# A hybrid decoder layer whose instruction order is planned at build time: other costs in the planner for POOL's inversion, the landing of stores and transfers in flight

## The chip, the cores and the metric

The kernel runs on one core of one Trainium2 chip. The metric is the device time of one execution in microseconds (us). A core has five engines with queues of their own: PE (matmuls; PEld in the profile is its weight load), DVE and ACT (elementwise work), POOL (elementwise work on SBUF alone) and SP, which here issues every transfer. Each engine works through its instructions in the order in which the program holds them and waits at semaphores for the others. So the order in which the instructions are written down decides what waits.

## The reference

One layer over 4096 tokens of width 1024: an RMS norm, one input projection `u = h @ w_in`, two groups of heads on its columns, a gate, an output projection with the residual, and a final RMS norm.

```
S_t = diag(a_t) S_{t-1} + k_t^T v_t ;  o_t = q_t S_t                              # GLA, 4 heads, 64 x 128
S_t = S_{t-1} (diag(w_t) - kk_t^T (a_t * kk_t)) + v_t^T k_t ;  y_t = S_t r_t       # RWKV-7, 8 heads, 64 x 64
x = x + concat(gla_out * silu(gg), (y + bonus) * silu(rg)) @ w_out
```

The inputs of the projections are float32; the kernel computes them with pairs of float16 numbers.

## The kernel before, in words

**Tiling.** The tokens go through in 8 blocks of 512. A projection (`proj`) is 24 float16 matmuls of 128x512: 8 slices of the width, three times, for the products of high and low halves of x and weight. Weights come as 29 column tiles of w_in and 8 of w_out. In the first block each tile is loaded as float32, its maximum is found (ACT `wo<-x`, then a transpose on PE, `bank<-ident,amW`), it is scaled and split into two float16 halves (`split_w`, line 604), and the halves are stored to DRAM (`wdr<-wo`, 512 KB; `wdr<-wr` and `wdr<-wg` for the first twelve). From the thirteenth tile on, the split works in two buffers `hls` (`wo` in the profile), so a store must have landed before the tile after the next can be split. Later uses load the halves from `wdr` into `wr`, `wg` or `wo` (256 KB each).

**RWKV.** Each block has four units, each of two heads, 32 units u = 4*b + p in all. `rwkv_ab` (line 833) projects, builds DD and bk on DVE, and multiplies them within chunks of 64 tokens (`bank<-DD,bk`); the masked products go to DD and Nb. DD and Nb have two buffers (`NBUF = 2`, line 525): unit u writes those of unit u-2, and line 881 lets it go on only when the scan of u-2 is written down. Then comes an inversion of triangular 32x32 blocks: four stores of 32 KB (`nd<-Nb`), four loads of 128 KB (`f<-nd`) that bring the rows to their partitions, 31 steps of two operations on POOL (`tm<-Tc,f`, `Tc<-Tc,tm`, lines 923 and 925), four stores `td<-Tc` and four loads `Nb<-td`. The last unit has its steps on DVE. `rwkv_i` (line 980) finishes the inverse with a transpose on DVE (`Ta<-Nb`) and small matmuls (`bank<-Ta,Nb`). `rwkv_c` (line 1002) is the scan over the 8 chunks of a unit: three float32 matmuls a chunk into `ch`, with ACT and DVE between them, then y (`y<-DD,sv`, `y<-Nb,uv`). `rwkv_d` (line 1046) normalises y; small rows go through DRAM to be spread over partitions (`bcast`, line 692: `bcda`, `bcdb`, `bcdc`, ...).

**The rest.** GLA's heads run beside that (`gla_proj`, `gla_pair`), `x_block` (line 739) prepares the next block's x, with its squares added up on POOL (`xacc`), and `out_block` (line 1240) does the output projection of a finished block.

**The order.** Every operation is recorded, not issued, by `Engine` (line 367, the issuing call is line 408, which is why every row of the profile has this line). Eight generators, one for each of the streams above, are run against a clock of costs (`run`, line 428), which fixes the buffers and the dependencies. Then a list scheduler plans all five engines: `forward` (line 245) goes through the steps by rank with a duration and a lag for each, `backward` (line 306) makes ranks from the far end, and this is repeated 13 times; the order with the earliest end by its own account is kept. All steps are then issued in the order of their planned starts. `cost` (line 334) has the durations for POOL ("G"), DVE ("V") and ACT ("S"). A transfer ("D") occupies its issuer for 0.63 us, begins 1.28 us later, lasts its bytes at 360 GB/s, and its reader may start a lag after that, with `SPARE` (0.45 us) on top.

In the built program the transfers use eight semaphores in turn, and each transfer waits until the eighth before it has landed.

Of the kernel before, what the change touches and what calls it, by code (L numbers as in the profile page):

```python
# [18 lines left out]
DRAM = bass.MemoryType.DRAM  # L19
# [62 lines left out]
def hymba_kernel(ctx, tc, xT, wt, wg, wo, wua, gup, pk, ck, out):  # L82
# [7 lines left out]
    big = ctx.enter_context(tc.tile_pool(name="big", bufs=1))  # L90
# [97 lines left out]
    steps, wkey, rkey, wlast, readers = [], {}, {}, {}, {}  # L188
# [56 lines left out]
    def forward(rank):  # L245


        wait, can, free = {e: [] for e in "VSGTD"}, {e: [] for e in "VSGTD"}, dict.fromkeys("VSGTDH", 0.0)
        pes, tab, run = Array(), 0, None
        left, ready, start = [len(s.on) for s in steps], [0.0] * len(steps), [0.0] * len(steps)  # L250
        end = [0.0] * len(steps)
        for s in steps:
            if not s.on:
                heapq.heappush(wait[s.eng], (0.0, s.n))

        def soonest(e):
            t = pes.free if e == "T" else free["H" if e == "D" else e]
            return t if can[e] else max(t, wait[e][0][0]) if wait[e] else 1e18

        for _ in steps:  # L260
            e = min("VSGTD", key=soonest)
            t = soonest(e)
            while wait[e] and wait[e][0][0] <= t:
                n = heapq.heappop(wait[e])[1]
                heapq.heappush(can[e], (rank[n], n))
            if e == "T":
                x = next((x for x in can[e] if run and x[1] == run.n), None)
                x = x or min(heapq.nsmallest(12, can[e]), key=lambda x: x[0] - 2.0 * (steps[x[1]].form == pes.form))
                run = steps[x[1]].next
                can[e].remove(x)  # L270
                heapq.heapify(can[e])
            else:
                x = can[e][0]
                soon = []
                while e in "VS" and wait[e] and wait[e][0][0] <= t + 0.15:
                    r, n = heapq.heappop(wait[e])
                    soon.append((r, n))
                    if rank[n] + 2 * (r - t) < x[0]:
                        x = (rank[n] + 2 * (r - t), n)
                for y in soon:  # L280
                    if y[1] != x[1]:
                        heapq.heappush(wait[e], y)
                if x is can[e][0]:
                    heapq.heappop(can[e])
            s = steps[x[1]]
            t, d = max(t, ready[s.n]), s.d
            start[s.n] = t
            if e == "T":
                start[s.n], d = pes.put(t, d, s.cols, s.tiles)
                end[s.n] = start[s.n] + d  # L290
            elif e == "D":
                free["H"], free["D"] = t + 0.63, max(t + 1.28, free["D"]) + d
                end[s.n] = free["D"]
            else:
                if s.tab is not None:
                    d, tab = d + 1.3 * (s.tab != tab), s.tab
                end[s.n] = free[e] = t + d
            for m in s.to:
                lat = m.on[s]
                ready[m.n] = max(ready[m.n], start[s.n] if lat is None or lat < 0 else end[s.n] + lat)  # L300
                left[m.n] -= 1
                if not left[m.n]:
                    heapq.heappush(wait[m.eng], (ready[m.n], m.n))
        return start, end
# [29 lines left out]
    def cost(eng, op, ins, n, o, acc=False):  # L334

        big = [a for a in ins if math.prod(a.shape[1:]) > 1 or n == 1]
        few = len(ins) - len(big)
        psum = any(a.space == PSUM for a in ins)
        if eng == "V":
            fast = len(big) == 1 and not psum and op in ("tensor_scalar", "tensor_copy", "tensor_scalar_mul", "tensor_scalar_max")  # L340
            if op == "tensor_tensor_scan":
                return 0.068 + n / 480
            half = o.shape[0] < 128
            runs = 0.0
            if op == "copy_predicated":
                runs = 0.135 if half else 0.013
            elif n == 64:
                runs = 0.126
            elif n == 256 and half:
                runs = 0.122 if op == "transpose" else 0.09  # L350
            elif n == 512 and half:
                runs = 0.115
            elif op == "tensor_scalar" and few > 1:
                runs = 0.06
            return 0.068 + 0.06 * (few > 0) + n / (1920 if fast else 960) + runs
        if eng == "G":
            if op == "memset":
                return 0.135 + n * 0.52 / 960
            return 0.14 + 0.07 * few + n * (2.13 if len(big) > 1 else 0.95) / 960 + 0.34 * (n == 8)
        if n <= 4:  # L360
            return 0.1 if n == 1 else 0.03
        if n == 64 and o.shape[0] == 64:
            return 0.231 if psum else 0.147
        d = (0.052 if psum else 0.094) + n / 1200 + 0.09 * (few > 0) + 0.11 * (o.shape[0] < 128)
        return d + (0.035 + 0.05 * (few > 1) if few and psum and n > 128 else 0.02 * (few > 0)) + 0.1 * acc

    class Engine:
# [5 lines left out]
        def __getattr__(self, op):  # L373
            f = getattr(self.eng, op)

            def call(*a, **kw):
                aps = [x for x in list(a) + list(kw.values()) if isinstance(x, bass.AP)]
                cols, tiles, tab, lag = 0, None, None, 0.2
                assert aps
                if aps:  # L380
                    o, ins, outs = aps[0], aps[1:], aps[:1]
                    n = max(math.prod(x.shape) // max(x.shape[0], 1) for x in aps)
                    if self.name == "T":
                        r = ins[-1] if op == "matmul" else ins[0]
                        n = math.prod(r.shape) // r.shape[0] if op == "matmul" else r.shape[0]
                        n *= (4 if op == "matmul" else 2) if r.dtype == F32 else 1
                        k = [(x.start_partition() // 32, (x.start_partition() + x.shape[0] + 31) // 32) for x in (ins[0], o)]
                        k.append((1 + (op == "matmul")) * (r.dtype == F32))
                        d, lag, cols, tiles = n / 2400 + 0.0025, 0.25, n * r.shape[0] / 128, k
                        t0 = account("T", o, ins, d, lag, cols, tiles)  # L390
                    elif self.name == "D":
                        b = math.prod(o.shape) * (2 if o.dtype == F16 else 4)
                        d, lag = max(0.01, b / 3.6e5), 1.6 if ins[0].space == DRAM else 0.6
                        t0 = account("D", o, ins, d, lag)
                    else:
                        e = kw.get("accum_out")
                        ins = [x for x in ins if x is not e]
                        outs = [o] + ([e] if e is not None else [])
                        d = cost(self.name, op, ins, n, o, e is not None)
                        if op == "activation" and a[2] in (AF.Ln, AF.Exp, AF.Tanh):  # L400
                            tab = int(a[2] == AF.Ln)
                        load = 1.2 * (tab is not None and tab != table[0])
                        table[0] = table[0] if tab is None else tab
                        t0 = account(self.name, o, ins, d + load, lag)
                        if e is not None:
                            for k in parts(e):
                                ready[k] = (ready[parts(o)[0]][0] + 0.1, self.name)
                put(t0, self.name, d, lag, cols, tiles, tab, outs, ins, lambda: f(*a, **kw))  # L408

            return call  # L410
# [1064 lines left out]
    with tc.manual_schedule(engines={getattr(mybir.EngineType, e) for e in ("PE", "DVE", "Activation", "Pool", "SP")}):  # L1475
# [6 lines left out]
        start, end = forward([s.t0 for s in steps])  # L1482
        start, end = best = forward(backward(end))
        for _ in range(12):
            start, end = forward(backward(end))
            best = min(best, (start, end), key=lambda x: max(x[1]))
        start, end = best
# [65 lines left out]
```

## Time and profile before

| | us |
|---|---|
| median of 3 runs (2348.07 to 2359.25) | 2356.71 |
| the profiled execution | 2357.35 |
| its span, first to last instruction | 2355.5 |
| PE busy | 2245.6 |
| DVE busy | 1664.7 |
| ACT busy | 1251.0 |
| POOL busy | 842.1 |

The mean granted clock of PE is 0.979 of full speed. How to read the lines below: a group has the line, the engine, the operation, the tiles out<-in (buffer numbers left out), shapes, the count, then busy us and mean ns of one, then the engine's idle time just before it and what ended it. In a list of waits there follow total us, number of times and the longest. In a table by stretch each engine has busy us with its instructions, then the granted clock, the share of the transfer engines in use and GB/s. In the chain of waits a transfer's piece runs from issue to landing. SPq is SP's own queue.

### The profile page before, as it was taken

How to read it: one execution, taken by the hardware profiler on the slowest of the kernel's cores; microseconds unless marked ns; L12 is line 12 of the kernel's file. 1: busy time of each engine (PE TensorE's matmuls, PEld its weight loads, DVE VectorE, ACT ScalarE, POOL GpSimd, SP SyncE). 2: the span in 40 equal slices, each digit the busy share in tenths (PEclk: the TensorE clock that was granted, in tenths of full speed). 3: DMA queues.
4: the chain of work that ended last, by engine and by line, in shares of the span. 5: the costliest groups of instructions: out<-in, count | busy, mean ns of one | idle time of the engine just before them, and what ended most of it. 6: DMA issues, size and time to landing. Idle time of an engine off the chain costs nothing.

```text
span 2355.5 us, 52166 instructions
## 1 busy us (share of the span) xinstructions
PE 2245.6 (95%) x19432; PEld 1390.7 (59%) x19432; DVE 1664.7 (71%) x3737; ACT 1251.0 (53%) x3229; POOL 842.1 (36%) x2213
## 2 busy tenths in 40 slices
PE   6888999999999999999999999999999989999986
PEld 3556565556665666656575566655666556755643
DVE  7868768478764786757766787638877677676756
ACT  7566765454654655544654546535564455544442
POOL 3450333524334352235425342342514353321400
PEclk9989999999999999999999999999999999999989
DMA  6666545355334543345424553345533454334432
GB/s 195 204 217 213 158 154 157 113 169 152 103 106 125 179 151 93 109 137 174 141 85 121 175 160 97 102 133 173 153 94 106 123 184 137 97 118 127 130 86 76
DMA packets 275523, 325.46 MB, mean 138 GB/s; under 512 B 131732, under 2 KB 132932, under 8 KB 275268
## 3 DMA queue, kind: packets, MB, share of 16 engines
q1 hardware_dynamic: 275268, 322.13, 45.0%
q8 instruction: 152, 2.49, 0.4%
q14 instruction: 103, 0.84, 0.1%
HBM read 276.97 MB, written 45.05 MB: 137 GB/s over the span
## 4 chain that ended last, share of the span: by engine, by line
PE 68%; DVE 19%; DMA 5%; issue 3%; ACT 2%; POOL 2%; SPq 1%; DVEq 0%; ACTq 0%; POOLq 0%
PE bank L408 60%; PE ch L408 6%; PE y L408 2%; DVE DD L408 2%; DVE nta L408 2%; DVE bk L408 1%; POOL tm L408 1%; POOL Tc L408 1%; DVE mgg L408 1%; DVE mgr L408 1%; SPq L408 1%; DMA wdr<-wo 1%; DVE Nb L408 1%; DVE crs L408 1%; DVE sv L408 1%
## 5 line engine op out<-in xcount | busy, mean ns | idle before, releaser
L408 PE MATMUL bank<-x,wr 128*128 128x512 f16 x3264 | 803.1, 380 | 12.5 <-DVE rk L408 4.7
L408 POOL TENSOR_TENSOR tm<-Tc,f 128x60 f32<-128x60 f32 (+24 forms) x961 | 332.4, 346 | 762.3 <-DMA f<-nd 586.0
L408 PEld LDWEIGHTS <-wr 128*128 128x128 f16 x3264 | 317.0, 100 | 308.0 <-issue 21.4
L408 PE MATMUL bank<-x,wg 128*128 128x512 f16 x1536 | 389.6, 383 | 2.4 <-DMA wg<-wdr 2.0
L408 POOL TENSOR_TENSOR Tc<-Tc,tm 128x60 f32<-128x60 f32 (+24 forms) x961 | 341.6, 355 | 73.4
L408 PE MATMUL bank<-x,wo 128*128 128x512 f16 x1488 | 361.9, 384 | 0.6 <-ACT bk L408 0.6
L408 DVE SCALAR_TENSOR_TENSOR sv<-ch,PC,psd 64x64 f32<-64x64 f32 x448 | 126.2, 282 | 195.9 <-PE ch L408 191.0
L408 POOL TENSOR_TENSOR xacc<-xacc,xr 128x512 f32<-128x512 f32 x98 | 131.3, 1340 | 314.8 <-ACT xr L408 215.3
L408 PEld LDWEIGHTS <-wg 128*128 128x128 f16 x1536 | 148.5, 101 | 147.4 <-issue 11.6
L408 PEld LDWEIGHTS <-wo 128*128 128x128 f16 x1488 | 146.0, 101 | 139.9 <-issue 8.0
L408 PEld LDWEIGHTS <-x 128*128 128x128 f16 x3120 | 189.9, 100 | 27.6 <-issue 12.2
L408 PE MATMUL bank<-wg,x 128*128 128x128 f16 x3072 | 199.6, 222 | 4.5 <-DMA wg<-wdr 4.5
L408 ACT ACTIVATE psd<-sv,PC 128x128 f32<-128x128 f32 x256 | 102.2, 399 | 190.1 <-DVE sv L408 152.9
L408 ACT COPY uv<-ch 64x64 f32<-64x64 f32 x512 | 105.5, 206 | 120.5 <-PE ch L408 114.8
L408 ACT COPY us<-ch 64x64 f32<-64x64 f32 x512 | 105.3, 206 | 103.7 <-PE ch L408 93.3
L408 PEld LDWEIGHTS ch<-sv,DD 128*128 128x128 f32 x512 | 91.9, 192 | 49.3 <-DVE sv L408 20.3
L408 PEld LDWEIGHTS ch<-us,Nb 128*128 128x128 f32 x512 | 92.3, 192 | 40.0 <-ACT us L408 10.5
L408 PEld LDWEIGHTS ch<-uv,bk 128*128 128x128 f32 x512 | 92.4, 192 | 39.6 <-ACT uv L408 12.5
L408 PE MATMUL ch<-sv,DD 128*128 128x128 f32 x512 | 105.9, 289 | 8.7 <-DVE sv L408 6.6
L408 ACT ACTIVATE sa<-bank,mu_s 128x512 f32<-128x512 f32 x104 | 71.5, 688 | 73.5 <-PE bank L408 68.5
L408 PE MATMUL ch<-uv,bk 128*128 128x128 f32 x512 | 103.4, 284 | 4.1 <-ACT uv L408 4.0
L408 POOL MEMSET Tc<- 32x8 f32 (+1 forms) x160 | 23.7, 148 | 223.3 <-DMA td<-Tc 182.2
(332 smaller groups left out, 3670.9 us busy)
## 6 DMA issues: line engine op xcount, KB each, us to landing
wr<-wdr SPq DMA_DIRECT2D x256, 256.0 KB
wg<-wdr SPq DMA_DIRECT2D x184, 256.0 KB
xr<-in_xT_dram SPq DMA_DIRECT2D x176, 256.0 KB
wo<-wdr SPq DMA_DIRECT2D x128, 256.0 KB
f<-nd SPq DMA_DIRECT2D x128, 128.0 KB
x<-in_wt_dram SPq DMA_DIRECT2D x29, 512.0 KB
wdr<-wo SPq DMA_DIRECT2D x25, 512.0 KB
out_dram<-mgg SPq DMA_DIRECT2D x33, 256.0 KB
```

The lines of the kernel that those rows point to most:

```text
L408: put(t0, self.name, d, lag, cols, tiles, tab, outs, ins, lambda: f(*a, **kw))
```

## The change

Only the planner is changed; the generators that say what is computed are not.

- `cost`: an operation on POOL other than a memset takes 0.23 us instead of 0.14 ahead of its elements.
- The recording of a transfer: the lag after a store to DRAM was 0.6 us; it becomes 2.0 us for over 200 KB, 1.3 us where the last dimension is 32 (`nd<-Nb`, `td<-Tc`), and stays 0.6 us for the rest. The lag after a load from DRAM stays 1.6 us.
- `forward`: a transfer can't start before the eighth one ahead of it has ended, its lag included.

```diff
-        end = [0.0] * len(steps)
+        end, flight = [0.0] * len(steps), []
...
             elif e == "D":
+                if len(flight) > 7:
+                    start[s.n] = t = max(t, flight[-8])
                 free["H"], free["D"] = t + 0.63, max(t + 1.28, free["D"]) + d
                 end[s.n] = free["D"]
+                flight.append(end[s.n] + s.lag)
...
-            return 0.14 + 0.07 * few + n * (2.13 if len(big) > 1 else 0.95) / 960 + 0.34 * (n == 8)
+            return 0.23 + 0.07 * few + n * (2.13 if len(big) > 1 else 0.95) / 960 + 0.34 * (n == 8)
...
-                        d, lag = max(0.01, b / 3.6e5), 1.6 if ins[0].space == DRAM else 0.6
+                        d, lag = max(0.01, b / 3.6e5), 1.6 if ins[0].space == DRAM else 2.0 if b > 2e5 else 1.3 if o.shape[-1] == 32 else 0.6
```

The first and last of these reach the generators' run as well as the list scheduler; the limit on transfers is in `forward` alone.

## The prediction

> **What bounds the kernel now.** I read the totals of the page first, then busy time by stretch, then the waits of PE, and last SP and POOL, which the change is about.
>
> ```profile
> span 2355.5 us, 52166 instructions
> PE 2245.6 (95%) x19432; PEld 1390.7 (59%) x19432; DVE 1664.7 (71%) x3737; ACT 1251.0 (53%) x3229; POOL 842.1 (36%) x2213
> ```
>
> ```profile
> core 0: us, PE busy (x) PEld busy (x) DVE busy (x) ACT busy (x) POOL busy (x), PEclk, DMA share, GB/s
> 0.00:200.00 200.00, 162.66 (x1124) 95.10 (x1126) 157.38 (x442) 132.68 (x256) 82.21 (x179) 0.92 0.68 211
> 200.00:2200.00 2000.00, 1955.94 (x17214) 1217.87 (x17210) 1409.35 (x3044) 1064.88 (x2826) 738.53 (x1979) 0.99 0.45 135
> 2200.00:2355.50 155.50, 126.98 (x1104) 77.76 (x1102) 97.96 (x253) 53.49 (x149) 21.37 (x55) 0.90 0.28 83
> ```
>
> PE is the bound: it stands idle for 37.3 us in the first 200 us (200 less 162.66), 44.1 in the 2000 in the middle and 28.5 at the end, 109.9 in all. The granted clock costs something beside that: 8% of the 162.66 busy us of the start, 1% of the 1955.94, 10% of the 126.98, 45 us together. So a microsecond of PE idle goes with some 0.4 us of lower clock (45 by 109.9), and a change of order can win or lose only in these two sums. What ends PE's longer idle stretches:
>
> ```profile
> PE bank L408 <- DVE bk L408: 14.7, 10, 4.3
> PE bank L408 <- ACT wo L408: 11.6, 6, 5.9
> PE bank L408 <- DMA wg<-wdr: 6.5, 4, 2.9
> PE bank L408 <- POOL xacc L408: 3.7, 2, 3.4
> PE bank L408 <- DVE Ta L408: 2.4, 3, 1.8
> PE bank L408 <- DMA wr<-wdr: 1.2, 1, 1.2
> ```
>
> The columns are total us, times and longest. Nothing is large, and the consumer of the inversion (Ta) is nearly absent.
>
> **The change part by part.** No instruction is added or removed. In the two built orders each engine holds the same operations, and PE the same 14,756 matmuls; all that moves is their order. So the cost has to come from what stands closer to what. I measure distances in *PE work*: the matmuls that stand between two instructions in the built order, each at the mean time PE gave to its group in the trace, idle left out.
>
> *POOL's inversion.* Each unit has 62 operations, and the edit adds 0.09 us to each: 5.6 us a unit. The old formula sums to 17.5 us, the new one to 23.1. The trace, for one unit and for all:
>
> ```profile
> L408 POOL TENSOR_TENSOR tm<-Tc,f x31: 209/296/1066, 584.3 to 610.5; 128x60 f32<-128x60 f32 x3, 128x28 f32<-128x28 f32 x2, 128x54 f32<-128x54 f32 x2, 128x48 f32<-128x48 f32 x2
> L408 POOL TENSOR_TENSOR tm<-Tc,f 128x60 f32<-128x60 f32 (+24 forms) x961 | 332.4, 346 | 762.3 <-DMA f<-nd 586.0
> L408 POOL TENSOR_TENSOR Tc<-Tc,tm 128x60 f32<-128x60 f32 (+24 forms) x961 | 341.6, 355 | 73.4
> ```
>
> ```profile
> L408 DVE STREAM_TRANSPOSE Ta<-Nb 32x256 f32<-32x256 f32 x64 | 27.6, 431 | 1.3
> L408 DVE TENSOR_TENSOR DD<-r,EP 64x512 f32<-64x512 f32 x64 | 46.5, 726 | 13.4 <-PE y L408 10.4 <-ACT EP L408 1.8
> ```
>
> The unit at 584.3 takes 26.2 us from first to last start, 21.7 of it busy on average (332.4 + 341.6 over 31 units). The new formula is closer to the truth. But the old one cost little: DVE waited 1.3 us in the whole run ahead of its transposes of the inverse, PE 2.4 us behind them. The reason stands in the old order itself: from the first store of nd to the last load of the inverse it already has 57.1 us of PE work on average (units 1 to 30). The new order has 67.9. These 10.8 us are taken from elsewhere: from the end of a unit's reads of DD for y to the first product of the unit that reuses the buffer, two units later, the distance falls from 17.8 to 10.3 us on average, and it is under 6.6 us for ten units instead of four. The 6.6 us are what DVE needs there:
>
> ```profile
> L408 DVE TENSOR_TENSOR bk<-kf,E 64x512 f32<-64x512 f32 x64 | 46.2, 722 | 3.8 <-PE ch L408 2.4
> L408 DVE SCALAR_TENSOR_TENSOR r<-r,pkt,kf 128x512 f32<-128x512 f32 x32 | 26.2, 818 | 0.1
> L408 DVE TENSOR_TENSOR DD<-rn,EP 64x512 f32<-64x512 f32 x64 | 45.4, 709 | 0.8
> L408 DVE SCALAR_TENSOR_TENSOR bk<-ta,E 64x512 f32<-64x512 f32 x64 | 46.7, 730 | 1.5
> ```
>
> Two each at 0.726, 0.722, 0.709 and 0.730 and one at 0.818 make 6.59. Already in the old order DVE waits 10.4 us there for y. The shortfall under 6.6 us, summed over units, grows from 5.2 to 19.9. The price lies between nothing (some of these operations can run ahead of the wait) and 14.7 us.
>
> A constant per operation is not what the trace shows of POOL, though:
>
> ```profile
> 125.31 1.21 POOL L408 TENSOR_TENSOR tm<-Tc,f 128x49 f32<-128x49 f32 x1
> 126.97 0.27 POOL L408 TENSOR_TENSOR tm<-Tc,f 128x42 f32<-128x42 f32 x1
> 125.10 1.28 DVE L408 SCALAR_TENSOR_TENSOR wo<-x,scl,wo 128x1024 f16<-128x1024 f32 x1
> ```
>
> The operation that starts inside DVE's 1.28 us takes 1.21 us and its neighbour 0.27. The Trainium skill (SBUF — State Buffer, Who interferes with whom) has the rule: a DVE instruction with two SBUF inputs and a GpSimd one that reads SBUF exclude each other for a whole instruction. This pair agrees; by that rule the added 0.09 us is an average that fits no unit in particular, and the sum stays.
>
> *Stores.* A store of over 200 KB now lands 1.4 us later in the model, one of 32-wide blocks 0.7 us. Issue to landing, from the chain of waits:
>
> ```profile
> 135.96 5.02 DMA wdr<-wo
> 162.62 6.36 DMA wdr<-wo
> 181.83 5.29 DMA wdr<-wo
> 376.68 3.94 DMA nd<-Nb
> ```
>
> The old model gives a 512 KB store 1.28 + 1.46 + 0.6 = 3.3 us, the new one 4.7, so again nearer. It matters in the start, where these stores free the two buffers of the weight split and the 11.6 us behind wo arise. In that stretch (up to 190 us of PE work in the order) the waits of PE on other engines whose distance is below the producer's duration plus 0.25 us fall short by 62.0 us together instead of 69.7: 11% less. Yet both orders put 161.5 us of PE work ahead of the last weight's maximum, so nothing new fills the start. I take 11% of its 37.3 us: -4.1; the bounds are -11.6 and 0.
>
> *The middle and the end* by the same measure: from 190 to 2140 us the shortfall rises from 436.2 to 461.8 (5.9%; within it bk falls from 21.8 to 10.5 and xacc from 6.9 to 4.7, others gain), at the end from 40.1 to 41.1. On 44.1 and 28.5 us of idle that is +2.6 and +0.7. The bounds are -15 (all waits for wg, wr, POOL and 40% of those for bk gone) and +25.6.
>
> *Eight in flight.* SP's waits in the first 30 us:
>
> ```profile
> SPq L408 <- DMA x<-in_wt_dram: 2.4, 4, 0.9
> SPq L408 <- DMA mgr<-in_xT_dram: 0.7, 2, 0.6
> SPq L408 <- DMA xr<-in_xT_dram: 0.6, 1, 0.6
> ```
>
> These are nearly all the waits of SP for the landing of an unrelated, earlier transfer: 3.7 us, in the start. Over the whole run SP waits for computing engines:
>
> ```profile
> SPq L408 <- PE bank L408: 524.1, 306, 8.6
> SPq L408 <- POOL Tc L408: 211.1, 47, 14.3
> ```
>
> So the limit itself is worth about nothing; it and the longer landings shift SP's order. Weight transfers with less than 3.5 us of PE work between issue and use are 44 instead of 31. In the old order such loads cost PE 7.7 us (6.5 + 1.2), 0.25 each; 13 more make +3.2, between 0 (a load may be issued early) and 20 (1.54 each, 7.7 over the five waits seen).
>
> *Array shapes.* PE changes the tile shape 648 times instead of 633. The price of a change is bounded by 0 and the 0.22 us before this weight load; I take 0.1, +1.5.
>
> ```profile
> 121.26 1.22 PEld L408 LDWEIGHTS bank<-vt,gbc 128*64 128x64 f32 x16 [0.22 <-issue]
> ```
>
> **The sum.** Idle: -4.1 + 2.6 + 0.7 + 3.2 = +2.4; with the clock, times 1.4, +3.4; shapes +1.5: **+4.9 us**. The hand-off of DD is within the middle's 2.6. The profiled execution took 2357.35 us, 1.85 above its span and 0.64 above the median of the three runs shown (2356.71), so the forecast is 2357.35 + 4.9 = 2362.
>
> The Trainium skill (TensorE: Matmul & The Clock Gate, What's actually happening) says that the clock halves only after an idle window of some 3.4 us. The waits I add are shorter (0.25 to 1.54); by that rule the factor of 1.4 goes and the sum is 2361. The row of the middle (44.1 us idle in short pieces, 1% lost) leans to the rule.
>
> **The rivals.** (1) *The mended waits go:* the 11.6 us behind wo, 3.7 for POOL and 7.7 for weights, 23.0 in all, with the clock 32; half of it gives 2341. For it: the model is nearer to the trace in all three. Against it: the start is held by the split's own chain of stores. (2) *The hand-off of the doubled DD becomes the wait:* DVE holds unit u+2's products until y of unit u has read DD, and PE waits for bk. Full price 14.7 times 1.4, 20.6 us: 2378. It decides from the point where the distance is under 6.6 us and the nine DVE operations can't start early. For it: the ten units, and the 10.4 us that exist. Against it: the four short ones of the old order show no long wait of their own. (3) *Nothing arrives:* POOL and the queue were never on PE's path, the distances change on both sides and even out: 2357, give or take 6.
>
> **How the numbers follow.** A measurement of this kernel can tell about 0.5% from no change, 11.8 us: faster is below 2345.6, slower above 2369.1. The forecast has 0.34, rival (3) 0.12, rival (1) 0.20, rival (2) 0.34. So faster 0.20, same 0.46, slower 0.34. The forecast's own range is 2350 to 2372. The range reaches past half of rival (1) to 2334 and past rival (2), with ten of the 20 us for tight loads, to 2388; I leave out the low end, 2325, where everything mended is won.
>
> **What would show it.** Right: PE busy within 5 us of 2245.6; its wait for wo below 11.6; DVE's wait for y ahead of DD above 10.4; DVE's idle before Ta still a few us; waits for wg and wr above 7.7. Rival (2): PE's wait for bk above 25. Rival (1): PE idle in the first 200 us below 27 with the middle not above 44. Wrong altogether: idle of the middle beyond 70 us from a wait not named here.

## The result and the profile after

The changed kernel takes 2385.1 us, median of four runs (2381.46 to 2388.29); the kernel before takes 2356.72 in the same comparison. The ratio is **1.0122, 95% interval 1.0097 to 1.0146**: slower by 28 us, where 5 were forecast. The profiled execution took 2384.56 us.

The totals of the page of after, then its busy time by stretch (columns as in the prediction):

```profile
span 2382.8 us, 52203 instructions
PE 2258.0 (95%) x19432; PEld 1390.1 (58%) x19432; DVE 1686.9 (71%) x3737; ACT 1247.2 (52%) x3229; POOL 838.8 (35%) x2213
```

```profile
0.00:200.00 200.00, 159.93 (x1094) 89.89 (x1094) 154.93 (x432) 130.91 (x252) 80.75 (x174) 0.94 0.67 204
200.00:2200.00 2000.00, 1948.87 (x17036) 1206.42 (x17037) 1414.04 (x3009) 1049.11 (x2785) 733.58 (x1972) 0.99 0.45 133
2200.00:2382.80 182.80, 149.23 (x1304) 93.75 (x1301) 117.92 (x297) 67.16 (x193) 24.49 (x67) 0.89 0.32 97
```

PE stands idle for 40.1 us in the start (37.3 before), 51.1 in the middle (44.1) and 33.6 at the end (28.5): 124.8 in all, 14.9 more. Its busy time rose by 12.4 with the same 19,432 matmuls. Together that is the 27.3 us by which the span grew. (The issuing line is 411 in the changed kernel and 408 before, since three lines were added above it.) The next row of after has a mean of 382 ns for the commonest matmul (380 before), while the starts of two such matmuls in an unbroken row lie 216 ns apart in both traces. A matmul that starts up to 0.16 us late (380 less 216 ns) still touches the end that the profile gives to the one before it, so the gap counts as busy.

```profile
L411 PE MATMUL bank<-x,wr 128*128 128x512 f16 x3264 | 807.2, 382 | 9.6 <-ACT x L411 2.3 <-DMA wr<-wdr 1.6 <-ACT E L411 1.6
```

The rows of 128x512 matmuls are not where the time went: added up from start to start over the whole trace, the steps from one 128x512 matmul to the next take 1246.4 us before and 1247.8 after, and all other steps 1095.9 and 1121.6. So 25.7 of the 27.3 us stand in steps with a smaller matmul at one end. Half of the loss shows as idle time. What the other half is, waits too short to show or something else that the order changes, these views do not settle. What ends the visible part, from the waits of PE of after (total us, times, longest):

```profile
PE ch L411 <- DVE sv L411: 9.7, 14, 1.9
PE bank L411 <- DVE DD L411: 8.8, 6, 4.2
...
PE bank L411 <- DVE bk L411: 7.8, 9, 1.5
PE bank L411 <- ACT wo L411: 7.4, 8, 1.9
PE bank L411 <- DVE tm L411: 6.1, 1, 6.1
PE bank L411 <- DVE pw L411: 4.9, 2, 3.7
PE bank L411 <- DVE lr L411: 4.7, 2, 4.5
...
PE bank L411 <- DMA wg<-wdr: 4.3, 5, 1.7
...
PE bank L411 <- DVE Ta L411: 3.9, 9, 1.0
...
PE bank L411 <- POOL xacc L411: 1.9, 1, 1.9
```

The rows of before for sv (the state that DVE writes after each chunk of the scan) and DD, which the prediction did not show:

```profile
PE ch L408 <- DVE sv L408: 6.6, 11, 1.8
...
PE bank L408 <- DVE DD L408: 2.9, 3, 2.2
```

No row has grown above 10 us. The waits that the edits aimed at are smaller (wo 7.4 after 11.6, xacc 1.9 after 3.7), and so is the one of rival (2) (bk 7.8 after 14.7). What grew is the sum of the waits for DVE: 25 rows in this view, from the 9.7 for sv downward, add up to 66.3 us; the 15 rows of before, from the 14.7 for bk downward, to 46.7. A few of them are long: 4.5 us for lr, 4.2 for DD and 3.7 for pw in the first 200 us, and 6.1 for tm near the end, in the last unit, whose inversion runs on DVE. The groups of DVE around the hand-off and the inverse, and SP's two longest waits:

```profile
L411 DVE TENSOR_TENSOR DD<-r,EP 64x512 f32<-64x512 f32 x64 | 51.0, 797 | 11.2 <-PE y L411 9.8
L411 DVE TENSOR_TENSOR bk<-kf,E 64x512 f32<-64x512 f32 x64 | 46.9, 733 | 7.7 <-PE ch L411 6.2 <-ACT E L411 0.5
L411 DVE STREAM_TRANSPOSE Ta<-Nb 32x256 f32<-32x256 f32 x64 | 27.5, 430 | 1.1
```

```profile
SPq L411 <- PE bank L411: 621.0, 348, 10.6
...
SPq L411 <- POOL Tc L411: 91.0, 35, 8.7
```

DVE's wait for y ahead of DD is as before (9.8 after 10.4), and its wait for the transposes' input is small (1.1). SP waits 91.0 us for the inversion's result instead of 211.1. That goes with the new price of POOL: the wait is 85.8 us with this price alone and 231.7 with the two lags alone.

### The profile page after: what moved, and what is told of

It is laid out like the page before. It is cut to its first block, busy times and chain, and to the rows that moved or that the text cites. A ratio compares the mean times of both kernels' runs of the same rounds, so it can differ in the third digit from the quotient of the medians.

```text
span 2382.8 us, 52203 instructions
## 1 busy us (share of the span) xinstructions
PE 2258.0 (95%) x19432; PEld 1390.1 (58%) x19432; DVE 1686.9 (71%) x3737; ACT 1247.2 (52%) x3229; POOL 838.8 (35%) x2213
## 4 chain that ended last, share of the span: by engine, by line
PE 49%; DVE 9%; DMA 2%; ACT 2%; POOL 2%; issue 1%; SPq 0%; DVEq 0%; ACTq 0%
PE bank L411 43%; PE ch L411 4%; PE y L411 2%; DVE DD L411 1%; DVE nta L411 1%; DVE bk L411 1%; POOL xacc L411 1%; DVE Nb L411 1%; DVE mgr L411 1%; POOL Tc L411 0%; DMA xr<-in_xT_dram 0%; POOL tm L411 0%; DVE mgg L411 0%; ACT x L411 0%; DMA crs<-bcdc 0%
## 5 line engine op out<-in xcount | busy, mean ns | idle before, releaser
L411 POOL TENSOR_TENSOR tm<-Tc,f 128x60 f32<-128x60 f32 (+24 forms) x961 | 324.4, 338 | 671.9 <-DMA f<-nd 542.6
L411 PEld LDWEIGHTS <-x 128*128 128x128 f16 x3120 | 190.5, 99 | 24.8 <-issue 10.2
L411 PEld LDWEIGHTS ch<-us,Nb 128*128 128x128 f32 x512 | 90.3, 192 | 40.1 <-ACT us L411 12.4
```

## The experiments

Three theories were held against each other. **The hand-off:** only the price of POOL and the lags together move DD's reuse up to 10.3 us of PE work, and that costs. **The stretched inversion:** the plan gives the inversion more room, SP issues its transfers later, and the real unit becomes longer, with weight loads squeezed together (those issued with under 3.5 us of PE work to their use rise from 31 to 44). Later this was sharpened to the *loop theory*: two buffers tie unit u+2 to unit u, and a longer unit eats the slack of that loop. **A redraw:** any new price draws another order, and orders differ by a per cent.

All ratios are to the kernel before in the same call, with 95% intervals.

| kernel | median us | ratio |
|---|---|---|
| POOL's price alone | 2350.55 | 0.997 [0.9956, 0.9984] |
| both lags alone | 2378.05 | 1.0091 [1.0067, 1.0116] |
| limit of eight alone | 2368.59 | 1.0048 [1.0032, 1.0063] |
| POOL's price 0.145 | 2360.04 | 1.0007 [0.9991, 1.0022] |
| POOL's price 0.135 | 2353.21 | 0.9954 [0.9935, 0.9974] |
| small lag alone | 2410.84 | 1.0197 [1.0172, 1.0222] |
| large lag alone | 2351.61 | 0.9954 [0.994, 0.9969] |
| POOL's price 0.32 | 2400.82 | 1.0169 [1.0145, 1.0193] |
| POOL's price and large lag | 2338.72 | 0.9906 [0.9889, 0.9922] |
| changed, small lag taken out | 2331.1 | 0.9878 [0.9859, 0.9897] |
| before, half the inversion's steps | 2338.34 | 0.9899 [0.988, 0.9919] |
| changed, half the inversion's steps | 2310.0 | 0.9787 [0.9772, 0.9802] |

The "small lag" is the 1.3 us of 32-wide blocks (nd and td), the "large lag" the 2.0 us of stores over 200 KB.

### The three edits, one at a time

POOL's price alone:

```diff
-            return 0.14 + 0.07 * few + ...
+            return 0.23 + 0.07 * few + ...
```

> POOL's 0.23 us alone; lags and the limit as before. In its order the unit's inversion (first store of nd to last load of the inverse) has 62.5 us of PE work (before 57.1, after 67.9) and the hand-off of DD from y of a unit to the products two units later 16.3 us (17.8, 10.3). Theory A, the longer planned inversion squeezes the hand-off and the scan: both are hardly squeezed, so 2357 to 2365. Theory B, late landings and tight loads (35 loads under 3.5 us; 31 before, 44 after): 2357 to 2362. Theory C, any change of a cost draws another order and the time scatters: anywhere within 25 us of 2357, without relation to these distances.

Both lags alone:

```diff
-  d, lag = max(0.01, b / 3.6e5), 1.6 if ins[0].space == DRAM else 0.6
+  d, lag = max(0.01, b / 3.6e5), 1.6 if ins[0].space == DRAM else 2.0 if b > 2e5 else 1.3 if o.shape[-1] == 32 else 0.6
```

> The longer landing of stores alone. Inversion 61.1 us of PE work, hand-off 16.3 us, 44 loads under 3.5 us as in the changed kernel. Theory A: 2357 to 2365, since the hand-off is hardly squeezed. Theory B: most of the loss, 2370 to 2385. Theory C: anywhere within 25 us of 2357.

The limit alone:

```diff
+                if len(flight) > 7:
+                    start[s.n] = t = max(t, flight[-8])
```

> The limit of eight transfers alone. Inversion 57.5 us of PE work, hand-off 17.7 us, 38 loads under 3.5 us. Theory A: 2355 to 2360. Theory B: 2357 to 2370 by its tight loads. Theory C: anywhere within 25 us of 2357.

A price that means nothing, 0.145 for 0.14:

```diff
-            return 0.14 + 0.07 * few + ...
+            return 0.145 + 0.07 * few + ...
```

> A change that means nothing: POOL's 0.14 us becomes 0.145 us, 0.3 us a unit. It tells how far the time moves when the order alone is drawn anew. Theory A and B: 2352 to 2362. Theory C: off by 10 us or more.

Measured: 0.997, 1.0091, 1.0048 and 1.0007. The three together (-0.3, +0.9 and +0.5%) make 1.1% and the change 1.2%, so no interplay of the three is needed to explain the loss. The hand-off theory falls: the lags lose alone, with 16.3 us of PE work at the hand-off in their order against 17.8 before and 10.3 in the changed one. The lags carry most of it.

### Which lag, how much POOL, and how wide the redraw is

```diff
-  ... else 0.6
+  ... else 1.3 if o.shape[-1] == 32 else 0.6
```

> Of the stores' landing only the part of nd and td (1.3 us where the last dimension is 32); large stores stay at 0.6 us. 46 loads with under 3.5 us of PE work to their use (before 31, e_lag 44), inversion 61.2 us. Theory B, loads for DVE and PE get closer to their use when the planner stretches the inversion: most of e_lag's 20 us, 2368 to 2380. Theory C, redraw: no relation to e_lag, 2345 to 2380.

```diff
-  ... else 0.6
+  ... else 2.0 if b > 2e5 else 0.6
```

> Of the stores' landing only the part of over 200 KB (2.0 us). Large stores are waited for in the start alone. 28 loads under 3.5 us, inversion 56.6 us. Theory B: nothing lost in the middle, some won or lost in the first 200 us, 2350 to 2362. Theory C: 2345 to 2380.

```diff
-            return 0.14 + ...
+            return 0.135 + ...
```

> A second change that means nothing, the other way: POOL's 0.14 us becomes 0.135 us. Theory B: 2352 to 2362 (32 loads under 3.5 us). Theory C: 10 us or more off.

```diff
-            return 0.14 + ...
+            return 0.32 + ...
```

> POOL's 0.14 us becomes 0.32 us, so that a unit has 28.7 us, what the trace shows from first to last operation. If SP's blocked time at td (211 us before, 86 in e_pool) is what e_pool won by: it falls further and the time is 2342 to 2352. If a stretched inversion costs (66.2 us of PE work, 49 loads under 3.5 us, hand-off 14.9 us): 2365 to 2385 as in the changed kernel.

The small lag alone loses 48 us by the medians (the kernel before took 2362.5 in that call), more than the whole change; the large one alone gains 11. A meaningless price moved the time by +0.1 and by -0.5%. So a gain of 0.3 to 0.5% of one edit is no more than a redraw, and the 2% of the small lag is four times the larger of the two redraws; two are few, and a wider scatter is not excluded by them. A price of 0.32 for POOL, which covers a unit's inversion from first to last operation and not only its busy time, loses 1.7%. In this kernel, too, SP's wait for Tc is short (71.4 us), so that wait is not what decides. Of the whole kernels whose count of tight weight loads is given here, the four with 44 to 49 lose 0.9% or more, and those with 28 to 38 lie between -0.9 and +0.5%. The count goes with the loss, but PE's own waits for wg and wr do not: they add up to 3.6 to 8.5 us in the four losers and to 7.7 before.

The waits of PE in the kernel with the small lag alone, the top rows and its totals:

```profile
span 2399.7 us, 52149 instructions
...
PE 2261.2 (94%) x19432; PEld 1389.0 (58%) x19432; DVE 1661.0 (69%) x3737; ACT 1248.2 (52%) x3229; POOL 842.6 (35%) x2213
```

```profile
PE ch L408 <- DVE sv L408: 18.4, 22, 2.7
PE bank L408 <- DVE amo L408: 10.0, 6, 5.6
PE bank L408 <- ACT wo L408: 8.9, 7, 4.0
PE bank L408 <- DVE bk L408: 8.7, 11, 2.3
PE bank L408 <- DVE DD L408: 7.2, 9, 2.4
```

PE is idle for 138.5 us here (2399.7 less 2261.2; 109.9 before) and its waits for DVE, 22 rows of this view, add up to 69.4 us (46.7 before); those for ACT make 50.2 (38.5 before). The wait for sv is the largest, nearly three times the 6.6 us of before.

### Half an inversion

If the loop is what hurts, a shorter inversion must take the pain away. Both kernels again, with this edit:

```diff
-        for j in range(31):
+        for j in range(0, 31, 2):
```

> The kernel before, with every second step of the inversion left out (16 steps instead of 31 in each unit), so the output is not the reference's. In before a unit takes 123.0 us from its first product with DD to the end of its scan, and 15.4 us remain until DD of the unit after the next; 27.9 of the 123.0 are the inversion on POOL. Both theories: some 14 us leave the unit's chain. Loop theory (the chain of two units is nearly as long as its two periods, and small stalls come where its slack goes): here the chain is 107 to 112 us with 25 or more to spare, and the time is 2335 to 2355. Theory of tight loads (weight loads issued with under 3.5 us of PE work to their use, 34 here against 31): 2355 to 2365.

> The changed kernel with the same steps of the inversion left out (16 instead of 31 in each unit), so the output is not the reference's. To be read against the kernel before with the same steps left out. Loop theory: with 14 us more slack in the chain of two units the four edits cost little: less than 10 us more than that kernel. Theory of tight loads (38 here against 34) and of a redrawn order: the loss does not hang on the length of the inversion: 15 to 28 us more than that kernel. Should the limit of eight in flight still cost at the start, as when made alone, 5 to 10 us of the difference stand in the first 400 us.

The page of before and then of the changed kernel, each with half the steps:

```profile
span 2344.1 us, 51219 instructions
...
PE 2240.0 (96%) x19432; PEld 1396.9 (60%) x19432; DVE 1654.7 (71%) x3707; ACT 1249.7 (53%) x3229; POOL 506.0 (22%) x1283
```

```profile
span 2306.8 us, 51228 instructions
...
PE 2223.9 (96%) x19432; PEld 1381.5 (60%) x19432; DVE 1651.1 (72%) x3707; ACT 1249.1 (54%) x3229; POOL 500.6 (22%) x1283
```

Two waits of PE, of before and then of the changed kernel, each with half the steps:

```profile
PE bank L408 <- ACT wo L408: 19.1, 10, 4.6
PE bank L408 <- DVE bk L408: 16.2, 10, 5.3
```

```profile
...
PE bank L411 <- ACT wo L411: 7.0, 7, 2.3
PE bank L411 <- DVE bk L411: 5.8, 7, 2.1
```

The sign turns round. With the long inversion the change costs 1.2%; with the short one it gains 1.1% (0.9787 by 0.9899, 0.9887, interval 0.986 to 0.991), and PE's idle time is 82.9 us (2306.8 less 2223.9) against 104.1 (2344.1 less 2240.0). So the cost of the change as a whole hangs on the length of the inversion. The theory that tight loads cost by themselves falls: the changed order has more of them (38 against 34) and is the faster one. Neither theory foresaw a gain of 28 us. Much of it is what the other edits win: the waits for wo and bk, 35.3 us together, fall to 12.8, and with the long inversion the change without its small lag gains nearly the same 1.2% (next section). That fits a small lag that costs nothing where the inversion is short, but no run has the small lag alone there. In the kernel before with half the steps the unit became 118.9 us long instead of the 107 to 112 expected: the scan, from its first product with the inverse to its end, took 50.7 us where it had taken 44.3.

### Without the small lag

The two edits that gained alone:

```diff
-            return 0.14 + ...
+            return 0.23 + ...
...
-  ... else 0.6
+  ... else 2.0 if b > 2e5 else 0.6
```

> POOL's price of 0.23 and the 2.0 us lag of stores over 200 KB, without the lag of 32-wide blocks and without the limit of eight. If the two edits add up as they did alone (0.997 and 0.995): 0.990 to 0.995 of before, 2334 to 2347. Loop theory: SP asks for the inversion's result at the right time (its wait for Tc below 100 us instead of 211.1) and the loads of f follow the stores of nd as early as before (9 to 10 us), so the unit's chain stays below 125 us: at most as long as before. Theory of tight loads: 30 with under 3.5 us against 31: as before within 0.5%. If the lag of the small blocks was not what lost, but any step away from the old order is: above 2365.

And the changed kernel with nothing but the small lag taken out (against the changed kernel):

```diff
-  ... else 2.0 if b > 2e5 else 1.3 if o.shape[-1] == 32 else 0.6
+  ... else 2.0 if b > 2e5 else 0.6
```

> The changed kernel without the 1.3 us lag of 32-wide blocks: POOL's price, the lag of the large stores and the limit of eight remain. Loop theory with the small lag as the culprit: SP asks for f as early as before (9 to 10.5 us after the store of nd, against 12.6 in the changed kernel), the unit's chain comes down from 128.8 to at most 125.5 us, and the time is that of the kernel with POOL's price and the large lag (0.991) plus what the limit of eight cost alone (0.005): 0.992 to 1.000, 2340 to 2362. If the price of POOL is what stretches the chain in the changed kernel (SP's last loads 15.1 us behind the inversion's end, against 8.5), and the small lag costs only in another company: the chain stays above 127 us and the time above 2372.

Measured: 0.9906 and **0.9878**: the second, at 2331.1 us, is the fastest whole kernel of this study, and beats both the kernel before and the changed one (0.9878 by 1.0122, 0.976). The small lag thus costs 2.0% alone, 1.4% beside the large lag (1.0091 by 0.9954) and 2.5% beside the other three prices (1.0122 by 0.9878). Three contrasts with the same sign, each several times the largest redraw seen, are hard to put down to a redraw. The page and the waits of PE of the changed kernel without it:

```profile
span 2329.6 us, 52178 instructions
...
PE 2240.0 (96%) x19432; PEld 1382.6 (59%) x19432; DVE 1667.8 (72%) x3737; ACT 1250.0 (54%) x3229; POOL 848.9 (36%) x2213
```

```profile
PE bank L411 <- DVE DD L411: 7.4, 9, 2.1
PE bank L411 <- ACT wo L411: 7.1, 8, 1.5
PE ch L411 <- DVE sv L411: 6.6, 10, 1.0
PE bank L411 <- DVE bk L411: 6.4, 4, 3.3
```

PE is idle for 89.6 us. The wait for wo keeps what the edits won (7.1), and the waits for DVE are back to 48.2 us (20 rows).

What the lag does in the trace is seen in SP's queue. This is the timeline of SP of the changed kernel, from the first store of nd of unit 15 to the first load of f (start us, duration, engine, tiles):

```profile
1127.67 0.40 SPq L411 DMA_DIRECT2D nd<-Nb  x1
...
1132.97 0.50 SPq L411 DMA_DIRECT2D crs<-bcdc  x1
1133.56 0.52 SPq L411 DMA_DIRECT2D xacc<-bcdx  x1
1134.14 0.48 SPq L411 DMA_DIRECT2D crs<-bcdc  x1
1134.67 0.57 SPq L411 DMA_DIRECT2D td<-Tc  x1
1135.29 0.45 SPq L411 DMA_DIRECT2D nd<-Nb  x1
...
1140.17 0.86 SPq L411 DMA_DIRECT2D f<-nd  x2
```

The same unit without the small lag:

```profile
1102.75 0.32 SPq L411 DMA_DIRECT2D nd<-Nb  x1
...
1110.24 0.35 SPq L411 DMA_DIRECT2D xr<-in_xT_dram  x1
1110.63 0.43 SPq L411 DMA_DIRECT2D nd<-Nb  x1
1111.11 0.45 SPq L411 DMA_DIRECT2D td<-Tc  x1
1113.39 0.31 SPq L411 DMA_DIRECT2D f<-nd  x1
```

With the lag 12.5 us pass, without it 10.6. The means over units 3 to 29, from the same starts (the last column is for the whole run):

| kernel | other transfers between first nd and f | first nd to f, us | inversion's end to first load of Nb, us | DD's first product to end of scan, us | PE's waits for DVE, us |
|---|---|---|---|---|---|
| before | 6.4 | 9.9 | 8.5 | 123.0 | 46.7 |
| changed | 9.1 | 12.6 | 15.1 | 128.8 | 66.3 |
| both lags alone | 8.2 | 12.0 | 10.2 | 127.2 | 67.4 |
| small lag alone | 8.2 | 12.0 | 10.7 | 127.8 | 69.4 |
| large lag alone | 7.1 | 10.5 | 8.6 | 122.3 | 48.6 |
| POOL's price alone | 7.4 | 10.4 | 11.6 | 124.7 | 45.8 |
| limit of eight alone | 6.6 | 9.9 | 8.5 | 123.1 | 61.6 |
| POOL's price 0.145 | 6.7 | 10.1 | 8.8 | 121.0 | 54.3 |
| POOL's price 0.135 | 7.2 | 10.7 | 8.1 | 122.8 | 44.7 |
| POOL's price 0.32 | 7.0 | 9.8 | 15.1 | 129.2 | 71.4 |
| POOL's price and large lag | 7.0 | 10.6 | 12.3 | 126.1 | 48.8 |
| changed, small lag out | 6.8 | 10.4 | 11.9 | 125.0 | 48.2 |
| before, half the steps | 5.1 | 10.2 | 10.8 | 118.9 | 43.8 |
| changed, half the steps | 7.4 | 12.4 | 15.0 | 118.6 | 37.7 |

In every whole kernel with the small lag SP puts 8.2 to 9.1 other transfers among and behind the stores of nd, and asks for f 12.0 to 12.6 us after the first of them; without the small lag it is 6.4 to 7.4 transfers and 9.8 to 10.7 us. With the lag and without, f is asked for on average 0.3 to 1 us after the last store of nd has landed, so it is mainly the stores themselves that came late: in the changed kernel SP spends 8.9 us from the first to the last of the four, without the small lag 7.4. The reading that fits: a planner that believes in a longer landing fills that time with other work, and SP, which works in order, really does that work first. No view here shows the plan's own times, so this step is argued.

Where PE's idle time and its waits for DVE stand, in the three stretches of the table by stretch (start, middle, end):

| kernel | PE idle, us | PE's waits for DVE, us |
|---|---|---|
| before | 37.3, 44.1, 28.5 | 12.3, 22.3, 12.2 |
| changed | 40.1, 51.1, 33.6 | 20.7, 26.4, 19.0 |
| small lag alone | 37.3, 65.7, 35.5 | 13.0, 41.2, 15.2 |
| changed, small lag out | 33.7, 30.7, 25.2 | 15.0, 22.0, 11.3 |

With the small lag alone the extra waits for DVE stand in the middle, where the loop of the units runs. In the changed kernel most of them stand in the start and at the end; against the same kernel without the small lag, though, the middle has 20.4 us more idle time, the larger part of the 35.2 between the two.

What is settled: the small lag is the price that turns the change into a loss, it goes with a later f in SP's order, and the change as a whole loses only where the inversion is long. What is *not* settled: which of the two stores, nd or td, the lag costs by, for both had it together, and the last link, which wait on DVE or PE the late inverse ends in. The length of the unit alone does not rank the kernels: 126.1 and 125.0 us belong to kernels faster than before with its 123.0. The four kernels with units of 127 us and more all lose, but part of that length is the loss itself: 2% of 123 us are 2.5. With 0.32 for POOL it is not f that is late (9.8 us) but the load of the inverse (15.1). So a late f is one way to lose and not the only one.

## Why the prediction was right and wrong

The sign and the range held: slower, 2385.1 within 2334 to 2388. The forecast of 2362 was short by 23 us, and its own range, 2350 to 2372, was missed. That the wide range held is luck: it reached 2388 by the price of rival (2) and half the bound for tight loads, and neither is what the runs show. Of the five signs for being right, the wait for wo fell and DVE's idle time before Ta stayed small; PE's busy time, DVE's wait for y and the waits for weights did not come as said. Point by point:

- **Stores** is the step that failed. The prediction found the new landing times "again nearer" to the trace, for both sizes, and priced both lags in the start alone, at -4.1 us. The large lag may stand: alone it gains 0.5%, about a redraw. The 32-wide blocks were given no price of their own, and their lag costs 2.0% alone (48 us) and 2.5% in the changed kernel. It is nearer to the trace and still loses; that the planner used the longer gap to slip other transfers in ahead is the reading that fits.
- **The start.** The wait for wo fell as said (11.6 to 7.4), but PE's idle time rose from 37.3 to 40.1; other waits took its place, those for pw, lr and DD above all.
- **The middle and the end** (+2.6 and +0.7): 7.0 and, in an end stretch longer by 27.3 us, 5.1 more idle, and in the whole run 12.4 more of busy time. The measure behind it, distances too short for the producer, was well short: it gave 5.9% more idle time for the middle, and 16% came. The wait for sv, which grew most where the small lag stands alone (6.6 to 18.4), is not in the prediction's list.
- **Weight loads** (+3.2): wrong. PE's waits for wg and wr fell from 7.7 to 5.9 us although 44 loads are tight, and in the pair with half an inversion the kernel with more of them is the faster one.
- **The clock** (times 1.4): not borne out. The granted clock cost 6% of 159.93, 1% of 1948.87 and 11% of 149.23, 45.5 us, as against 45 before, though idle time rose by 14.9; whole per cents are too coarse to say more. Between other kernels the two do go together: the mean granted clock is 0.986 where PE is idle for 89.6 us (the small lag taken out) and 0.989 where it is idle for 82.9 (changed, half the steps), against 0.979 with 109.9 before. The Trainium skill (TensorE: Matmul & The Clock Gate, What's actually happening) has the clock fall only after an idle window of some 3.4 us. The trace does not decide it: the waits for sv are shorter (1.9 us at most), but five single waits are longer (3.7 to 6.1), as some were before (4.3 for bk, 5.9 for wo).
- **PE busy within 5 us** of 2245.6: it rose by 12.4. The Trainium skill (Perfetto Trace Analysis, Tensor Engine Instruction) says that a matmul's end is computed from its size and not seen; the trace agrees, with 382 ns given and 216 from start to start, and busy sums between 2223.9 and 2261.2 us for the same matmuls in the pages shown here.
- **Array shapes** (+1.5): no run changes the number of shape changes alone, so this term is neither shown nor refuted.
- **POOL's inversion.** That the old price cost little is right: the new one alone gives 0.997, no more than a redraw. That its stretched order costs by the hand-off is wrong: DVE's wait for y went from 10.4 to 9.8 us, and PE's waits for bk and DD together from 17.6 to 16.6.
- **Eight in flight** ("about nothing"): alone it costs 0.5%, 11 us; beside POOL's price and the large lag it costs nothing (0.9878 with it, 0.9906 without). Both differences are of the size of a redraw, so these runs name no price for it.
- **Rival (2)** gave 2378, near the result, for a reason that fell: PE's wait for bk is 7.8 us, not above 25. **Rival (1)**, the mended waits, was real but hidden by the small lag: without it the change gives 2331.1 with PE idle for 20.3 us less than before (89.6 against 109.9). The waits that this rival named, 23.0 us, fall to 8.4 there (7.1 for wo, 0.5 for POOL, 0.8 for wr).

## What to carry to other kernels

A planner's price is judged by the order it draws, not by how near it is to the trace: put each price in alone, and put a meaningless change of price beside it, so that you know what a redraw is worth (here up to 0.5%). A longer lag in the plan can let other transfers slip in ahead on a queue that works in order; here the kernels with that delay lost as long as the inversion was long. And where PE is nearly always busy, look into its busy sum too, from start to start: of 27.3 us lost here 12.4 stood in it.

## What the runs showed of the hardware

Matmuls of 128x512 in an unbroken row start 216 ns apart while each is shown as some 380 ns long. The same 19,432 matmuls have busy sums 37 us apart (2223.9 to 2261.2 in the pages shown here) in kernels that differ only in order and in work that is not PE's.
